# Differential heads: one VectorE instruction for the first softmax's scaling and the sum of both

## The chip, the cores and the metric

The kernel runs on one core of one Trainium2 chip. A core has five engines with a queue each: TensorE (PE in the profile; its weight loads are shown apart as PEld), VectorE (DVE), ScalarE (ACT), GpSimd (POOL) and SyncE (SP), which here issues most of the DMAs. Each engine works through its own instructions in a fixed order and waits on semaphores for the others.

The metric is the device time of one execution in microseconds (us); lower is better.

## The reference

The reference is one decoder block on a sequence of 1024 tokens with 1024 channels, float32. The input is normalised (RMS) and projected. Two attention branches follow: eight "forgetting" heads (FoX) of 64 channels, and four differential heads. Both are gated, merged by sigmoid gates, projected out, normalised and added to the input.

A differential head has two pairs of queries and keys, with rotary embedding, and one value of 128 channels. Its output is the difference of two causal softmaxes, times the value:

```
logits = einsum('bhmqd,bhmkd->bhmqk', qi, k) * scale        # m = 0, 1
p  = softmax(where(kpos <= qpos, logits, -inf))
pd = p[:, :, 0] - lam * p[:, :, 1]                          # lam: one number per layer
out = einsum('bhqk,bhkd->bhqd', pd, v)
```

## The kernel before, in words

Matrix products are made in a high and a low part: each float32 operand is split into a rounded part and the remainder, and three products (high x high, high x low, low x high) are summed.

The kernel goes through five stages: it loads and transposes x and makes the values (to about 100 us of the span); it works through eight attention units, units 0 to 3 being the differential heads and 4 to 7 pairs of FoX heads; then gates, branch products and the output projection.

In an attention unit the 1024 queries are taken in eight blocks of 128, called rows here (i = 0 to 7), in groups of two (g). The groups of one unit go up or down in order (GORD). Row i of a differential head has n = (i + 1) x 128 columns, and goes through these steps:

- s_row (line 449), once for each of the two softmaxes: two matmuls per piece of up to 512 columns write the scores to a PSUM tile Sd (lines 460, 461; three such tiles take turns); a VectorE instruction (line 463) scales them, adds the mask, writes them to a row buffer Pd in SBUF and finds the maximum (mxd); ACT takes the exponential in place and sums it (line 469) into one column of a small tile l. The row buffers come from a pool of six.
- row (line 550): VectorE takes the reciprocals of both sums (line 559, tile l). POOL multiplies the second row p2 with its reciprocal and with nlam, which is -lam (line 560). ACT multiplies the first row p1 with its reciprocal (line 562). POOL adds p2 to p1 (line 563).
- av (line 473): TensorE transposes blocks of p1 (line 490, tile ptd), ACT copies the high part (line 493, phd), VectorE makes the low part (line 494, pld), and TensorE multiplies with the value (line 514, ypd).

FoX rows have one softmax each: reciprocal on VectorE (line 590), scaling on POOL (line 591), no sum.

Beside the rows, TensorE has filler work in the same stretch: the projections of the next unit's queries and keys (line 301, tiles pq and pk) and of gate paths (pz). These bring work for the other engines: splitting the weights (hi on POOL, line 289; lo on VectorE, line 291), and for differential heads the rotary embedding: a copy on ACT (line 339), four DMAs that swap halves (line 343), a product on VectorE (line 345), a product on POOL (line 346, swq and swk), their sum on VectorE (line 347, rotq and rotk), and the split into the tiles TA, TB, KA, KB on ACT and VectorE (lines 352 to 355).

The order of instructions on each engine isn't the order in which the code is written. A planner works it out when the program is built, by simulating it with its own costs: what was written first has priority, and an engine takes the first instruction that is ready. A few orders are pinned by hand (issue_after). On the chip the order of each engine is then fixed.

Of the kernel before, what the change touches and what calls it, by code (L numbers as in the profile page):

```python
# [11 lines left out]
AF = mybir.ActivationFunctionType  # L12
ALU = mybir.AluOpType
# [31 lines left out]
def f32(ap):  # L45
    return ap.bitcast(F32)
# [3 lines left out]
def tile_hybrid_block(  # L50
# [18 lines left out]
    nc = tc.nc  # L69
# [237 lines left out]
    with ExitStack() as st:  # L307
# [127 lines left out]
        def swapped(T, m, g, nm):  # L435

            src = T["TB" if m else "TA"]
            qs = slice(2 * g * P, (2 * g + 2) * P)
            t = qk.tile([P, 2 * P], F32R, tag=f"X{m}", name=f"X{m}{nm}_{g}", bufs=3)
            for a, b in ((UPR, DNR), (DNR, UPR)):  # L440
                lastx[0] = nc.sync.dma_start(f32(t[a]), f32(src[b, qs])).ins
            if vload:
                with tc.issue_after(lastx[0]):
                    vload.pop(0)()
            return t
# [3 lines left out]
        def s_row(T, m, i, X, bias, boff, nm, le=None):  # L449

            A, B = (T["TA"], T["KA"]) if m == 0 else (T["TB"], T["KB"])
            n = (i + 1) * P
            qs = slice(i * P, (i + 1) * P)
            xs = slice(i % 2 * P, (i % 2 + 1) * P)
            pr = pp.tile([P, S], F32, tag="P", name=f"P{nm}_{m}_{i}")
            mx = small.tile([P, 2], F32, tag="mx", name=f"mx{nm}_{m}_{i}", bufs=8)
            pcs = pieces(i)
            for j, (a, b) in enumerate(pcs):
                ps = sps.tile([P, CH], F32, tag="S", name=f"S{nm}_{m}_{i}_{j}")[:, 0:b - a]
                nc.tensor.matmul(ps, lhsT=A[:, qs], rhs=B[:, a:b], start=True, stop=False)  # L460
                lasts[0] = nc.tensor.matmul(  # L461
                    ps, lhsT=X[:, xs], rhs=B[:, a:b], start=False, stop=True).ins
                nc.vector.tensor_tensor_reduce(  # L463
                    out=pr[:, a:b], in0=ps, in1=bias[:, boff + a:boff + b], scale=-0.125,
                    scalar=BIG if j == 0 else mx[:, j - 1:j], op0=ALU.add, op1=ALU.min,
                    accum_out=mx[:, j:j + 1])
            if le is None:
                le = small.tile([P, 1], F32, tag="l", name=f"l{nm}_{m}_{i}", bufs=8)
            nc.scalar.activation(pr[:, 0:n], pr[:, 0:n], AF.Exp,  # L469
                                 bias=mx[:, len(pcs) - 1:len(pcs)], scale=-1.0, accum_out=le)  # L470
            return pr, le
# [57 lines left out]
        def unit_attn(u, T):  # L529

            diff = u < 4
            t = u if diff else u - 4
            vt = qk.tile([P, NB, 256], F32R, tag="V", name=f"V{u}")
            src = (vb_d if diff else va_d)[:, t, :].rearrange("(b p) c -> p b c", p=P)
            cb = []
            groups = []

            def load_v():
                nc.sync.dma_start(f32(vt), src)

            def load():
                if not diff:
                    for m in range(2):
                        b = big.tile([P, S], F32, tag="big", name=f"cb{u}_{m}")
                        h = 2 * t + m
                        nc.sync.dma_start(b, cum_d[h:h + 1, :].to_broadcast([P, S]))
                        cb.append(b)

            if diff:
                def row(i, rows):  # L550
                    boff = S - (i + 1) * P
                    if "X" not in rows:
                        rows["X"] = [swapped(T, m, i // 2, f"d{u}") for m in range(2)]
                    le = small.tile([P, 2], F32, tag="l2", name=f"l{u}_{i}", bufs=4)
                    l1, l2 = le[:, 0:1], le[:, 1:2]
                    p1, _ = s_row(T, 0, i, rows["X"][0], dmask, boff, f"d{u}", l1)
                    p2, _ = s_row(T, 1, i, rows["X"][1], dmask, boff, f"d{u}", l2)
                    n = (i + 1) * P
                    nc.vector.reciprocal(le, le)  # L559
                    nc.gpsimd.tensor_scalar(  # L560
                        p2[:, 0:n], p2[:, 0:n], l2, nlam, op0=ALU.mult, op1=ALU.mult)
                    nc.scalar.activation(p1[:, 0:n], p1[:, 0:n], AF.Copy, scale=l1)
                    nc.gpsimd.tensor_tensor(
                        p1[:, 0:n], p1[:, 0:n], p2[:, 0:n], op=ALU.add)
                    rows[i] = p1

                def evac(g):
                    def run(yp):
                        ys = stg.tile([P, 2 * P], F32, tag="ys", name=f"ys{u}_{g}")
                        nc.scalar.copy(ys, yp)  # L570
                        nc.sync.dma_start(y_d[u][:, g * 2 * P:(g + 1) * 2 * P], ys)
                    return run

                for g in GORD[u]:
                    rows = {}
                    groups.append((
                        4 * g + 3,
                        [lambda i=i, rows=rows: row(i, rows) for i in (2 * g, 2 * g + 1)],
                        lambda g=g, rows=rows: av(rows, g, vt, 0, False, evac(g), f"d{u}_{g}", False)))
            else:  # L580
                ysb = {}

                def row(m, i, rows):
                    n = (i + 1) * P
                    diag = cb[m][:, n - P:n]
                    nc.gpsimd.tensor_tensor(diag, diag, trim, op=ALU.add)  # L586
                    if "X" not in rows:
                        rows["X"] = swapped(T, m, i // 2, f"f{u}")
                    p1, l1 = s_row(T, m, i, rows["X"], cb[m], 0, f"f{u}")
                    nc.vector.reciprocal(l1, l1)  # L590
                    nc.gpsimd.tensor_scalar(  # L591
                        p1[:, 0:n], p1[:, 0:n], l1, 1.0, op0=ALU.mult, op1=ALU.mult)
                    rows[i] = p1

                def evac(m, g):
                    def run(yp):
                        if m == 0:
                            ysb[g] = stg.tile([P, 2 * P], F32, tag="ys", name=f"ys{u}_{g}")
                        tmp = stg.tile([P, 2 * P], F32, tag="yt", name=f"yt{u}_{m}_{g}", bufs=1)
                        nc.scalar.copy(tmp[64:128], yp[64:128])  # L600
                        nc.vector.tensor_tensor(
                            ysb[g][64 * m:64 * m + 64], yp[0:64], tmp[64:128], op=ALU.add)
                        if m == 1:
                            nc.sync.dma_start(y_d[u][:, g * 2 * P:(g + 1) * 2 * P], ysb[g])
                    return run

                for g in GORD[u]:
                    for m in range(2):
                        rows = {}
                        groups.append((  # L610
                            4 * g + 3,
                            [lambda m=m, i=i, rows=rows: row(m, i, rows) for i in (2 * g + 1, 2 * g)],
                            lambda m=m, g=g, rows=rows: av(
                                rows, g, vt, m * P, True, evac(m, g), f"f{u}_{m}_{g}",
                                u == 7 and g in FING)))
            return load, load_v, groups
# [528 lines left out]
```

## Time and profile before

| | |
|---|---|
| time of three runs, median (lowest to highest) | 905.3 us (904.18 to 906.15) |
| the profiled execution's own time | 906.41 us |
| its span, first to last instruction | 904.6 us |
| granted TensorE clock | 0.998 |
| busy: PE, DVE, ACT, POOL | 883.2, 606.5, 439.5, 421.6 us |
| differential rows (tile Pd), first and last start | 138.5 to 358.8 us |

The span is what the profile covers; 1.8 us of the execution lie outside it. Busy time is the time in which an engine works on instructions; ends of matmuls are modelled, so that a busy PE can still lose time between matmuls. In a row of a group, "x32 | 24.7, 774 | 10.3" means 32 instructions, 24.7 us in all, 774 ns on average, and 10.3 us in which the engine stood idle just before them, with what ended that idle time. "A <- B: 3.5, 4, 1.5" means that A waited for B 3.5 us in total, 4 times, at most 1.5 us. "128x512" is partitions by elements.

### The profile page before, as it was taken

The numbers are of one execution on the slowest core, as the hardware profiler recorded it, in microseconds if no ns is written. First come the engines' busy times: TensorE is split into PE (matmuls) and PEld (weight loads), VectorE is DVE, ScalarE is ACT, GpSimd is POOL, SyncE is SP. The second block draws the span as 40 slices with busy tenths as digits, with TensorE's granted clock in tenths as the row PEclk, the third lists the DMA queues.
The fourth block names the chain that finished last, engine by engine and source line by source line (L and its number), as shares of the span: only waits on it lengthen the run. The fifth ranks groups of instructions, "written<-read, shape, count | busy, mean of one in ns | idle before, by whom it ended". The sixth has DMA issues, their size and how long they took to land.

```text
span 904.6 us, 13660 instructions
## 1 busy us (share of the span) xinstructions
PE 883.2 (98%) x4600; PEld 746.0 (82%) x4600; DVE 606.5 (67%) x1150; ACT 439.5 (49%) x878; POOL 421.6 (47%) x413
## 2 busy tenths in 40 slices
PE   7999999899999999999999999999999999999996
PEld 5899988688888888888888888888888888888885
DVE  6767556878668664557657557526586896648797
ACT  3433225576757675365555547534444362314342
POOL 7325324545546456154344446425634323483861
PEclk9999999999999999999999999999999999999999
DMA  9556747424336350432523532198766599210395
GB/s 321 191 169 257 277 114 196 112 76 124 108 70 185 76 181 19 140 85 76 163 59 88 152 89 71 40 405 264 229 201 203 199 306 339 73 45 0 118 194 177
DMA packets 129224, 140.09 MB, mean 155 GB/s; under 512 B 10353, under 2 KB 96369, under 8 KB 128130
## 3 DMA queue, kind: packets, MB, share of 16 engines
q1 hardware_dynamic: 124786, 136.87, 48.2%
q0 software_dynamic: 4224, 2.10, 2.0%
q8 instruction: 36, 0.59, 0.3%
q14 instruction: 34, 0.28, 0.1%
q10 hardware_dynamic: 144, 0.26, 0.1%
HBM read 86.17 MB, written 38.34 MB: 138 GB/s over the span
## 4 chain that ended last, share of the span: by engine, by line
PE 84%; DVE 5%; issue 3%; POOL 3%; DMA 2%; ACT 2%; SPq 1%; POOLq 0%; DVEq 0%; ACTq 0%
PE x_g L785 15%; PE pb L945 10%; PE pv L200 9%; PE x_o L785 9%; PE pz L301 8%; PE pk L301 7%; PE pq L301 7%; PE ypf L514 4%; PE ptf L490 3%; PE ypd L514 2%; PE Sd L460 2%; PE Sf L460 2%; PE Sf L461 1%; PE ptd L490 1%; PE Sd L461 1%
## 5 line engine op out<-in xcount | busy, mean ns | idle before, releaser
L200 PE MATMUL pv<-wvhi,hT 128*128 128x264 f32 (+2 forms) x384 | 88.8, 323 | 0.4 <-DVE hT L186 0.4
L301 PE MATMUL pz<-hT,hi_z 128*128 128x512 f32 x256 | 83.5, 397 | 0.2 <-ACT sq L418 0.2
L301 PE MATMUL pk<-hT,hi_k 128*128 128x512 f32 x256 | 82.3, 395 | 0.9 <-DVE KB L355 0.9
L301 PE MATMUL pq<-hT,hi_q 128*128 128x512 f32 x256 | 81.8, 394 | 0.0
L945 PE MATMUL pb<-yT,hi_br 128*128 128x512 f32 x256 | 78.8, 389 | 0.0
L785 PE MATMUL x_g<-T,a_g 128*128 128x512 f32 x336 | 78.0, 391 | 0.0
L785 PE MATMUL x_o<-wo_op,a_o 128*128 128x512 f32 x336 | 77.6, 392 | 0.0
L785 PEld LDWEIGHTS x_o<-wo_op,a_o 128*128 128x128 f32 x336 | 63.0, 188 | 14.5 <-DVE a_o L735 0.5
L785 PEld LDWEIGHTS x_g<-T,a_g 128*128 128x128 f32 x336 | 63.1, 188 | 13.8
L200 PEld LDWEIGHTS pv<-wvhi,hT 128*128 128x128 f32 x384 | 64.2, 189 | 6.1 <-DVE hT L186 0.7
L469 ACT ACTIVATE Pd<-Pd,mxd 128x128 f32<-128x128 f32 (+7 forms) x64 | 49.6, 775 | 35.6 <-DVE mxd L463 35.3
L586 POOL TENSOR_TENSOR cb<-cb,trim 128x128 f32<-128x128 f32 x64 | 31.3, 492 | 70.2 <-DVE mxf L463 51.8
L200 PE MATMUL pv<-wvlo,hT 128*128 128x512 f32 (+2 forms) x192 | 62.0, 325 | 0.7 <-DVE wvlo L156 0.7
L494 DVE TENSOR_TENSOR plf<-ptf,phf 128x512 fp32r<-128x512 f32 (+1 forms) x80 | 50.0, 635 | 17.7 <-ACT phf L493 16.7
L469 ACT ACTIVATE Pf<-Pf,mxf 128x1024 f32<-128x1024 f32 (+3 forms) x64 | 49.8, 778 | 24.4 <-DVE mxf L463 23.5
L591 POOL TENSOR_SCALAR Pf<-Pf,lf 128x1024 f32<-128x1024 f32 (+3 forms) x64 | 47.9, 753 | 27.9 <-DVE lf L590 25.6
L560 POOL TENSOR_SCALAR Pd<-Pd,l,nlam 128x128 f32<-128x128 f32 (+7 forms) x32 | 29.3, 916 | 66.1 <-DVE l L559 59.9
L785 PE MATMUL x_g<-hT,a_g 128*128 128x512 f32 x252 | 59.1, 392 | 0.0
L945 PEld LDWEIGHTS pb<-yT,hi_br 128*128 128x128 f32 x256 | 48.1, 188 | 9.9
L785 PEld LDWEIGHTS x_g<-hT,a_g 128*128 128x128 f32 x252 | 47.3, 188 | 10.5
L301 PEld LDWEIGHTS pk<-hT,hi_k 128*128 128x128 f32 x256 | 47.2, 188 | 10.3 <-DVE KB L355 1.5
L301 PEld LDWEIGHTS pq<-hT,hi_q 128*128 128x128 f32 x256 | 47.6, 188 | 9.2
(261 smaller groups left out, 2339.3 us busy)
## 6 DMA issues: line engine op xcount, KB each, us to landing
t_d<-t SPq DMA_DIRECT2D x16, 512.0 KB, 4.2
T<-t_d SPq DMA_DIRECT2D x8, 1024.0 KB, 10.5
raw<-in_w_in_dram SPq DMA_DIRECT2D x14, 512.0 KB, 4.9
vb_d<-vbs SPq DMA_DIRECT2D x8, 512.0 KB, 3.8
va_d<-vas SPq DMA_DIRECT2D x8, 512.0 KB, 5.2
raw_k<-in_w_in_dram SPq DMA_DIRECT2D x8, 512.0 KB, 5.3
raw_q<-in_w_in_dram SPq DMA_DIRECT2D x8, 512.0 KB, 4.2
V<-vb_d SPq DMA_DIRECT2D x4, 1024.0 KB
```

The lines of the kernel that those rows point to most:

```text
L200: nc.tensor.matmul(ps[n], lhsT=hT[hp][k // 4][i // 4][:, k % 4, hs], rhs=wt[k][:, a:b], start=first, stop=(k == KT - 1 and hp == 1))
L301: mm = nc.tensor.matmul(ps, lhsT=a[:, k, :], rhs=hT[h][k // 4][c][:, k % 4, :], start=(k == 0 and a is hi and h == 0), stop=(k == KT - 1 a ...
L460: nc.tensor.matmul(ps, lhsT=A[:, qs], rhs=B[:, a:b], start=True, stop=False)
L469: nc.scalar.activation(pr[:, 0:n], pr[:, 0:n], AF.Exp, bias=mx[:, len(pcs) - 1:len(pcs)], scale=-1.0, accum_out=le)
L490: lasts[0] = nc.tensor.transpose(pt[:, o * P:(o + 1) * P], rows[2 * g + r][:, j * P:(j + 1) * P], ident).ins
L494: nc.vector.tensor_tensor(pl[:, 0:n], pt[:, 0:n], ph[:, 0:n], op=ALU.subtract)
L514: lasts[0] = nc.tensor.matmul(o, lhsT=a, rhs=b[:, src], start=(j == 0 and n == 0), stop=(odd == 1 and jj == g and n == len(prods) - 1)).ins
L560: nc.gpsimd.tensor_scalar(p2[:, 0:n], p2[:, 0:n], l2, nlam, op0=ALU.mult, op1=ALU.mult)
L586: nc.gpsimd.tensor_tensor(diag, diag, trim, op=ALU.add)
L591: nc.gpsimd.tensor_scalar(p1[:, 0:n], p1[:, 0:n], l1, 1.0, op0=ALU.mult, op1=ALU.mult)
L785: nc.tensor.matmul(x[m], lhsT=a[:, ai, k, :], rhs=right[m][bi][k], start=(k == 0 and n == 0), stop=(k == 3 and n == 2))
L945: nc.tensor.matmul(ps, lhsT=a[:, kk, :], rhs=yT[g][h][:, k % 2, sl], start=(k == 0 and a is hi and h == 0), stop=(k == 3 and a is lo))
```

## The change

The scaling of the first row on ACT and the sum on POOL are replaced by one scalar_tensor_tensor on VectorE, which multiplies p1 with its reciprocal and adds p2, in place in p1. The scaling of p2 on POOL stays, and so do the reciprocals. All four differential heads are affected, 32 rows in all.

```
                     nc.vector.reciprocal(le, le)
                     nc.gpsimd.tensor_scalar(
                         p2[:, 0:n], p2[:, 0:n], l2, nlam, op0=ALU.mult, op1=ALU.mult)
-                    nc.scalar.activation(p1[:, 0:n], p1[:, 0:n], AF.Copy, scale=l1)
-                    nc.gpsimd.tensor_tensor(
-                        p1[:, 0:n], p1[:, 0:n], p2[:, 0:n], op=ALU.add)
+                    nc.vector.scalar_tensor_tensor(
+                        p1[:, 0:n], p1[:, 0:n], l1, p2[:, 0:n], op0=ALU.mult, op1=ALU.add)
                     rows[i] = p1
```

## The prediction

> **What bounds the kernel now.** I read the page's busy times first, then busy times by stretch, then the waits of the matmul engine and of VectorE inside the stretch that the change touches.
>
> ```profile
> PE 883.2 (98%) x4600; PEld 746.0 (82%) x4600; DVE 606.5 (67%) x1150; ACT 439.5 (49%) x878; POOL 421.6 (47%) x413
> ```
>
> TensorE is busy for 98% of the span, the others for 47 to 67%. That is an average, so the next view is by stretch. The differential rows (tile Pd) run between 138 and 345 us. The columns are busy us and count for PE, PEld, DVE, ACT, POOL, then the granted clock.
>
> ```profile
> 140.00:360.00 220.00, 215.12 (x1154) 181.14 (x1154) 156.12 (x368) 141.97 (x288) 119.85 (x104) 1.00 0.43 114
> 160.00:180.00 20.00, 17.27 (x86) 13.39 (x85) 17.68 (x32) 10.34 (x19) 10.80 (x8) 1.00 0.46 116
> 260.00:280.00 20.00, 19.99 (x114) 16.96 (x113) 16.97 (x36) 11.73 (x24) 11.20 (x9) 1.00 0.47 126
> 360.00:580.00 220.00, 217.70 (x1272) 188.65 (x1271) 136.61 (x365) 123.39 (x270) 94.24 (x135) 1.00 0.34 97
> ```
>
> In the differential stretch PE is idle for 220 - 215.12 = 4.9 us, and 20 - 17.27 = 2.7 us of that lies in the one slice 160 to 180, the slice where VectorE is at 17.68 / 20 = 88%. Over the whole stretch VectorE is at 156.1 / 220 = 71%. So TensorE sets the end and VectorE is next. What PE waits for there (columns: us in total, times, longest):
>
> ```profile
> PE Sd L460 <- DVE mxd L463: 3.5, 4, 1.5
> PE pk L301 <- DVE KB L355: 0.9, 1, 0.9
> PE ptd L490 <- POOL Pd L563: 0.4, 1, 0.4
> ```
>
> 4.4 of its 4.8 us are waits for VectorE, 0.4 us for the POOL sum that the change removes. PE does not wait for the ACT scaling at all. Whatever the change frees on POOL and ACT can therefore give back at most 4.8 us here, and only by way of VectorE.
>
> **What is removed.** 32 scalings on ACT and 32 sums on POOL, one of each for every differential row.
>
> ```profile
> L562 ACT ACTIVATE Pd<-Pd,l 128x128 f32<-128x128 f32 (+7 forms) x32 | 24.7, 774 | 10.3 <-DVE l L559 10.2
> L563 POOL TENSOR_TENSOR Pd<-Pd,Pd 128x128 f32<-128x128 f32 (+7 forms) x32 | 48.1, 1508 | 8.7 <-ACT Pd L562 5.9 <-issue 1.6
> L560 POOL TENSOR_SCALAR Pd<-Pd,l,nlam 128x128 f32<-128x128 f32 (+7 forms) x32 | 29.3, 916 | 66.1 <-DVE l L559 59.9 <-PE pz L301 4.3 <-ACT Pd L469 1.9
> ```
>
> ACT loses 24.7 us of 142.0, POOL 48.1 us of 119.9. Neither is close to full in this stretch and PE waits for neither, apart from the 0.4 us, so by themselves these 72.8 us are worth 0.4 us. What covers them is the matmul stream (215 of 220 us); without that cover a row's own path would count: after the reciprocal it is now max(916, 774) + 1508 = 2.42 us on average until the transposes may read the row.
>
> **What is added.** 32 scalar_tensor_tensor instructions on VectorE, widths 128 to 1024, both tensor inputs in SBUF. The stretch has none, but other stages have them at 128x512:
>
> ```profile
> L1071 DVE SCALAR_TENSOR_TENSOR go<-go,ors,mg 128x512 f32<-128x512 f32 x4 | 2.8, 747 | 1.1 <-POOL ors L1055 1.1
> L176 DVE SCALAR_TENSOR_TENSOR xg<-xs,rs,g_bc 128x512 f32<-128x512 f32 x16 | 13.2, 859 | 2.9 <-POOL rs L118 2.9
> L463 DVE CUSTOM_DVE_ANT_0 Pd<-Sd,dmask 128x512 f32<-128x512 f32 x32 | 21.8, 682 | 3.3 <-POOL Pd L563 1.9 <-PE Sd L461 1.3
> L463 DVE CUSTOM_DVE_ANT_0 Pd<-Sd,dmask 128x384 f32<-128x384 f32 x16 | 8.7, 551 | 4.9 <-PE Sd L461 3.6 <-POOL Pd L563 1.2
> ```
>
> The two widths of L463 differ by 682 - 551 = 131 ns for 128 columns. From 747 ns at 512 columns I get 354 ns at 128, 485 at 256, 616 at 384, 878 at 640 and 1271 at 1024: eight widths together 6.5 us, four heads 26.0 us, mean 812 ns. L176's mean instead of L1071's would add 32 x 0.11 = 3.6 us; I take L1071, the row nearest to L463's 682 ns for the same width, and price POOL's disturbance separately below. No DMA is issued, removed or moved by the change, so no queue of SP or POOL is passed. A row's path becomes 916 + 812 = 1.73 us, 0.7 us shorter, if VectorE is free when POOL is done.
>
> The Trainium skill (Vector Engine (DVE) Microarchitecture Reference, Points that are easy to get wrong) says that this instruction shape with two SBUF sources that are not bf16 runs at half throughput. L1071 has just such sources (go and mg are f32 in SBUF) and takes 747 ns against 682 ns for L463, which reads one input from PSUM: no halving here. By the rule the sum would be 52 us in place of 26.0 us.
>
> **VectorE against POOL.** Instructions of VectorE with two SBUF inputs get longer when POOL is already working. The rows, in order of time (start us, us):
>
> ```profile
> 151.66 0.69 DVE L355 TENSOR_TENSOR KB<-rotk,KB 64x512 fp32r<-64x512 f32 x1
> 155.23 1.49 DVE L347 TENSOR_TENSOR rotq<-rotq,swq 128x512 f32<-128x512 f32 x1 [1.48 <-POOL swq L346]
> 160.31 1.07 DVE L353 TENSOR_TENSOR TA<-rotq,TA 64x512 fp32r<-64x512 f32 x1
> 168.54 1.94 DVE L355 TENSOR_TENSOR KB<-rotk,KB 64x512 fp32r<-64x512 f32 x1
> ```
>
> ```profile
> 155.15 1.03 POOL L563 TENSOR_TENSOR Pd<-Pd,Pd 128x384 f32<-128x384 f32 x1
> 156.13 1.50 POOL L289 TENSOR_SCALAR hi_z<-raw_z 128x1024 fp32r<-128x1024 f32 x1
> 158.92 1.92 POOL L563 TENSOR_TENSOR Pd<-Pd,Pd 128x512 f32<-128x512 f32 x1 [0.31 <-ACT Pd L562]
> 167.96 1.97 POOL L563 TENSOR_TENSOR Pd<-Pd,Pd 128x640 f32<-128x640 f32 x1 [1.25 <-ACT Pd L562]
> ```
>
> Undisturbed it is 0.69 us (151.66). At 168.54 KB overlaps a POOL sum that ends at 169.93 and itself ends 0.55 us after that. So the second one stands until the first is done, and the POOL sums cost VectorE 0.80 + 0.38 + 1.25 = 2.43 us in this stretch alone. The new instruction comes under the same lock. It starts at the end of a POOL scaling, where POOL may have its next instruction ready and take the lock again. The nearest rows are the rope sums, also two-input instructions released by POOL:
>
> ```profile
> L347 DVE TENSOR_TENSOR rotk<-rotk,swk 128x512 f32<-128x512 f32 x8 | 7.9, 990 | 14.2 <-POOL swk L346 14.2
> L347 DVE TENSOR_TENSOR rotq<-rotq,swq 128x512 f32<-128x512 f32 x8 | 7.6, 946 | 9.0 <-POOL swq L346 9.0
> ```
>
> Their mean is 968 ns against 690, so 0.28 us each: 32 x 0.28 = 9.0 us for the new instructions at most by these rows, nothing at least. I take the upper end as nearest. The Trainium skill (SBUF — State Buffer, Who interferes with whom) calls it an exclusive lock between a VectorE instruction with two SBUF inputs and a GpSimd instruction that reads SBUF; by that rule, the trace agrees, it speaks against a change that puts 32 more such instructions on VectorE.
>
> **Waits that go and come.** VectorE itself waits in this stretch for the removed sum, because the sum holds the second softmax's buffer:
>
> ```profile
> DVE Pd L463 <- POOL Pd L563: 7.7, 4, 3.2
> DVE cum L646 <- POOL Pd L563: 1.4, 1, 1.4
> ```
>
> These 9.1 us end, for VectorE is then itself the last reader. In their place it waits for the POOL scaling L560, with the next rows' L463 reductions queued behind the waiting instruction, and PE's score matmuls behind those. The matching handoffs POOL to VectorE are the rope waits, 14.2 + 9.0 us over 16, mostly late DMA; the bound for 32 new waits is zero to 32 x 0.92 = 29 us (0.92 is L560's own time, as if VectorE always came at its start). I take near zero: the order of each engine is planned with the POOL scaling ahead.
>
> **The sum.** VectorE's work in the stretch goes from 156.1 to about 156.1 + 26.0 + 9.0, less the locks of the sums that go. That is near 186 to 191 us of 220, or 85 to 87%, like the slice 160 to 180 and the slice 260 to 280. Most of it falls where PE has matmuls to go on with. The place where VectorE leads PE is 155 to 171 us. There the rows of 384, 512 and 640 columns add 0.62 + 0.75 + 0.88 = 2.24 us and 3 x 0.28 = 0.84 us of lock; the locks of the sums give back 2.43 us (1.6 us if hi_z moves up and takes the first). With the 0.4 us that PE waited for the sum: 2.24 + 0.84 - 2.43 - 0.4 = +0.25 us, on the profiled execution's 906.4 us. That execution is 1.1 us above the median of 905.3 us, so the forecast is 905.6 us: no change that can be told (about 0.2%, or 1.8 us, is what a measurement of this kernel can tell).
>
> **Rivals.**
>
> *The freed POOL and buffer shorten the chain (faster).* The chain of waits around 193 to 219 us runs through the removed pair:
>
> ```profile
> 192.28 1.06 ACT Pd L562
> 193.48 2.39 POOL Pd L563
> ...
> 207.94 0.75 POOL Pd L563
> ...
> 217.39 1.27 POOL Pd L563
> ```
>
> Together 5.47 us; the new instructions for these widths (1024, 256, 512) take 1.27 + 0.49 + 0.75 = 2.5 us, 3.0 us less. For it: the 9.1 us of VectorE's buffer waits end as well. Against it: PE waited only 0.4 us for that chain. Time 905.3 - 3.0 = 902.3 us, at the very best 905.3 - 4.8 = 900.5 us.
>
> *VectorE becomes the bound (slower).* The place is 140 to 219 us, where that chain is mostly off PE. The price: twelve rows, one whole head and the first four of the next, put 6.5 + 2.2 = 8.7 us on VectorE, with 12 x 0.28 = 3.4 us of lock; the pieces above give back 5.47 us, so 8.7 + 3.4 - 5.47 = +6.6 us, or +4.2 us with the sums' locks (2.43 us) given back too. It decides once a scalar_tensor_tensor stands in VectorE's queue ahead of a reduction that PE's next score matmul waits for. For it: 3.5 of PE's 4.8 us are of this kind. Against it: in the slice 260 to 280 VectorE is at 16.97 / 20 = 85% and PE loses 0.01 us. Time 909.5 to 911.9 us.
>
> *The instruction runs at half rate (slower).* Each takes twice the time worked out from L1071, 8.7 us more in the same twelve rows: 905.3 + 4.2 + 8.7 = 918.2 us. L1071 itself speaks against it; 2%. It is what the Trainium skill's page on the VectorE microarchitecture, cited above, would make of the change.
>
> *The planner.* The order on each engine is worked out from the planner's own costs, so other lines move too, also behind the stretch, where 220 - 217.70 = 2.3 us of PE idle is all there is to win. This can blur each case by about 2 us either way.
>
> **How the numbers follow.** No change 36%, the chain shortened 30%, VectorE as the bound 32%, half rate 2%. That gives faster 0.30, same 0.36, slower 0.34. The likeliest's own range is 903.5 to 907.1 us; signs being nearly even, the range reaches to the best case, 900.5 us, and to the second's upper price, 911.9 us.
>
> **What would show it.** A group of 32 scalar_tensor_tensor on Pd at 0.81 us undisturbed, up to 1.09 us with locks; POOL busy in the stretch down by 48 us, ACT by 25 us, VectorE up by 26 to 35 us less 2 to 8 us; no wait of L463 for a POOL sum; PE's idle time in 140 to 360 still near 5 us. I am wrong if that idle time goes under 3 us or over 8 us, if VectorE's waits for L560 exceed 10 us, or if the stretches behind 360 us change by more than 2 us.

## The result, and the profile after

The changed kernel takes 914.48 us in the median of six runs (910.29 to 916.85), beside 905.67 us of six runs of the kernel before (904.18 to 908.15). The ratio is 1.0081, with a 95% interval from 1.0062 to 1.0100: slower. The ratio comes from the comparison of the runs and isn't quite the quotient of the two medians. Where I turn a ratio into us below, I multiply what it has over 1 by 905.8 us, a median of the kernel before: here +7.3 us (5.6 to 9.1). The profiled execution took 912.89 us, of which the span is 911.1 us, 6.5 us more than before. One of the ten runs of e4, an experiment below, took 2043.86 us, more than twice any other, and is left out of its median and ratio.

The page's busy times after, then busy times by stretch (columns as before: PE, PEld, DVE, ACT, POOL, granted clock):

```profile
PE 887.9 (97%) x4600; PEld 747.7 (82%) x4600; DVE 627.3 (69%) x1182; ACT 417.1 (46%) x846; POOL 373.9 (41%) x381
```

```profile
140.00:360.00 220.00, 212.58 (x1127) 176.75 (x1126) 173.52 (x392) 116.06 (x253) 70.52 (x68) 1.00 0.42 113
360.00:580.00 220.00, 217.98 (x1264) 188.40 (x1262) 136.64 (x363) 124.02 (x269) 95.74 (x138) 1.00 0.34 97
```

In the differential stretch POOL lost 119.85 - 70.52 = 49.3 us, ACT 25.9 us, and VectorE gained 17.4 us. Behind 360 us nothing moved. So the loss lies inside the stretch, and little of it shows as idle time of TensorE: its idle time over the whole span grew from 904.6 - 883.2 = 21.4 to 23.2 us, only 1.8 us. Its busy time grew by 4.7 us, with the same 4600 matmuls. Ends of matmuls are modelled, so a matmul that starts late can have a longer record, and small gaps vanish in it. To find the place I therefore compared starts. In each trace the matmuls were added up in order, each by its undisturbed spacing (0.227 us at 512 columns, 0.117 at 256, 0.060 at 128), and I looked at when each kernel had started the same amount of work:

```
work done before at (us)   34   137   158   183   205   249   270   292   315   337   537   end
after behind by (us)     +1.4  +1.4  +1.8  -0.5  -0.9  +0.6  +0.4  +4.9  +6.0  +6.4  +6.2  +6.5
```

The 1.4 us at 34 us are not the change: up to about 130 us the two have the same order of instructions, and other runs differ by as much there. In the first differential head the changed kernel even gains 2.3 us. By 270 us it is level. It then loses 5.6 us within 45 us, and hardly anything more. At 297 us, where the kernel before begins its fourth differential head, it is already 6.1 us behind, so the loss lies in the third. Busy times of the four heads, each from its first reciprocals (line 559) to the next head's, first before, then after:

```profile
146.00:201.00 55.00, 51.75 (x265) 41.76 (x264) 42.58 (x92) 34.26 (x69) 30.93 (x25) 1.00 0.46 119
201.00:246.00 45.00, 44.62 (x245) 38.20 (x244) 33.54 (x81) 30.42 (x64) 23.54 (x21) 1.00 0.44 117
246.00:297.00 51.00, 50.08 (x276) 42.60 (x275) 39.40 (x92) 34.48 (x73) 28.95 (x25) 1.00 0.45 118
297.00:344.00 47.00, 46.67 (x258) 39.73 (x257) 28.69 (x75) 32.16 (x65) 25.08 (x23) 1.00 0.42 120
```

```profile
147.00:204.00 57.00, 55.06 (x284) 45.50 (x283) 48.68 (x101) 29.41 (x61) 19.54 (x18) 1.00 0.46 119
204.00:256.00 52.00, 51.13 (x275) 42.92 (x274) 41.48 (x94) 27.79 (x64) 16.30 (x15) 1.00 0.39 105
256.00:303.00 47.00, 42.81 (x235) 34.76 (x233) 39.14 (x93) 26.04 (x58) 13.84 (x15) 1.00 0.45 120
303.00:350.00 47.00, 46.58 (x255) 39.37 (x254) 34.83 (x81) 24.37 (x53) 14.94 (x16) 1.00 0.42 120
```

TensorE's idle time in the third head goes from 0.92 to 4.19 us, while the first head's falls from 3.25 to 1.94 us. VectorE does not explain it by its share alone: in the third head it is at 39.14 / 47 = 83%, in the first at 48.68 / 57 = 85%. What differs is what TensorE has beside the rows. The projections alone (line 301; columns PE, PEld, clock), in the same heads, before and then after:

```profile
146.00:201.00 55.00, 37.73 (x145) 26.45 (x146) 1.00 0.46 119
201.00:246.00 45.00, 30.01 (x118) 21.32 (x117) 1.00 0.44 117
246.00:297.00 51.00, 32.82 (x128) 23.05 (x127) 1.00 0.45 118
297.00:344.00 47.00, 27.07 (x111) 20.14 (x110) 1.00 0.42 120
```

```profile
147.00:204.00 57.00, 42.40 (x163) 29.70 (x163) 1.00 0.46 119
204.00:256.00 52.00, 33.79 (x132) 23.68 (x130) 1.00 0.39 105
256.00:303.00 47.00, 23.36 (x89) 16.14 (x90) 1.00 0.45 120
303.00:350.00 47.00, 27.38 (x113) 20.37 (x111) 1.00 0.42 120
```

The number of projection matmuls goes 145, 118, 128, 111 before and 163, 132, 89, 113 after. With longer rows the planner fits more of them between the rows of the first two heads, and the third head is left with 39 fewer, 9.5 us of TensorE's work (its window is 4 us shorter, too). The third unit is the one that has none of the gate projection as filler of its own. A list in the kernel says which of its eight parts go to which unit:

```
ZFILL = ((0,), (1,), (), (2,), (3,), (4,), (5,), (6, 7))
```

There the chain of each row shows. The three longest waits of TensorE's matmuls in 280 to 303 us, in order of time (start us, us), and instructions of VectorE ahead of the first:

```profile
285.70 0.50 PE L460 MATMUL Sd<-KA,TA 128*128 128x512 f32 x1 [1.16 <-DVE mxd L463]
299.64 0.30 PE L490 MATMUL ptd<-ident,Pd 128*128 128x128 f32 x1 [0.95 <-DVE Pd L562]
300.60 0.39 PE L460 MATMUL Sd<-KB,TB 128*128 128x256 f32 x1 [0.66 <-DVE mxd L463]
```

```profile
280.83 0.89 DVE L562 SCALAR_TENSOR_TENSOR Pd<-Pd,l,Pd 128x640 f32<-128x640 f32 x1 [1.08 <-POOL Pd L560]
284.31 0.93 DVE L347 TENSOR_TENSOR rotq<-rotq,swq 128x512 f32<-128x512 f32 x1 [1.98 <-POOL swq L346]
285.16 0.47 DVE L463 CUSTOM_DVE_ANT_0 Pd<-Sd,dmask,mxd 128x256 f32<-128x256 f32 x1
```

The score matmuls (L460) wait for VectorE's reduction (L463) to release the PSUM tile, and the transposes (L490) for the new instruction. VectorE in turn has stood idle for POOL. Not all of that is the new instruction's doing. The reduction that the matmul of 285.70 us waits for stands behind a sum of the rotary embedding (L347, a rope sum), which waited 1.98 us for POOL's rope product, and that one 2.19 us for its DMA:

```profile
282.99 1.29 POOL L346 TENSOR_TENSOR swq<-swq,sinT 128x512 f32<-128x512 f32 x1 [2.19 <-DMA swq<-rawq]
```

By starts, 2.1 of the 5.6 us are lost just here (+1.3 us at 282 us, +3.4 us at 286). The kernel before (its rope sum at 281.74 us) and e1 and e3 below don't wait at this place; e5 waits 1.95 us. Whether the order or the DMA brings this wait was not tested.

The group of the new instruction in 138 to 365 us after:

```profile
L562 DVE SCALAR_TENSOR_TENSOR Pd<-Pd,l,Pd 128x128 f32<-128x128 f32 (+7 forms) x32 | 34.2, 1069 | 10.6 <-POOL Pd L560 10.4
```

The 32 new instructions take 34.2 us, 1069 ns each, and VectorE stands 10.4 us before them waiting for the POOL scaling, 13 times and at most 1.5 us. Some are long for the lock with POOL, as foreseen. This one, 128x1024 (1.27 us by the forecast's row), starts just behind a product of POOL:

```profile
194.26 2.32 DVE L562 SCALAR_TENSOR_TENSOR Pd<-Pd,l,Pd 128x1024 f32<-128x1024 f32 x1
```

```profile
194.20 1.30 POOL L346 TENSOR_TENSOR swk<-swk,sinT 128x512 f32<-128x512 f32 x1 [0.92 <-DMA swk<-rawk]
```

### The profile page after: what moved, and what is told of

Same layout as the page of the kernel before. It is cut to its first block, busy times and chain, and to the rows that moved or that the text cites. A ratio compares the mean times of both kernels' runs of the same rounds, so it can differ in the third digit from the quotient of the medians.

```text
span 911.1 us, 13604 instructions
## 1 busy us (share of the span) xinstructions
PE 887.9 (97%) x4600; PEld 747.7 (82%) x4600; DVE 627.3 (69%) x1182; ACT 417.1 (46%) x846; POOL 373.9 (41%) x381
## 4 chain that ended last, share of the span: by engine, by line
PE 82%; DVE 5%; DMA 3%; issue 3%; ACT 2%; SPq 2%; POOL 1%; DVEq 0%; POOLq 0%; ACTq 0%
PE x_g L784 15%; PE pv L200 10%; PE pb L944 10%; PE x_o L784 8%; PE pz L301 8%; PE pk L301 7%; PE pq L301 7%; PE ypf L514 3%; PE ptf L490 3%; PE ypd L514 2%; DMA swq<-rawq 2%; PE Sf L460 1%; PE Sf L461 1%; PE pg L301 1%; PE ptd L490 1%
## 5 line engine op out<-in xcount | busy, mean ns | idle before, releaser
L200 PE MATMUL pv<-wvhi,hT 128*128 128x264 f32 (+2 forms) x384 | 90.7, 328 | 0.8 <-DVE hT L186 0.8
L493 ACT CAST phf<-ptf 128x512 fp32r<-128x512 f32 (+1 forms) x80 | 42.6, 542 | 38.0 <-PE ptf L490 31.7
```

The costliest lines, as they stand in the source:

```text
L200: nc.tensor.matmul(ps[n], lhsT=hT[hp][k // 4][i // 4][:, k % 4, hs], rhs=wt[k][:, a:b], start=first, stop=(k == KT - 1 and hp == 1))
L493: nc.scalar.copy(ph[:, 0:n], pt[:, 0:n])
```

## The experiments

The theories were these. LOAD: VectorE's extra work costs time where TensorE has too little filler, whatever the work is. HANDOFF: VectorE stands behind POOL, first for the scaled p2 and then for the lock. HOLE: the place is the third head, because its unit has no gate filler; in the texts written before the runs this goes by the name of COVER, against LOAD EVERYWHERE, by which the loss follows VectorE's work wherever the filler stands. ORDER: adding instructions upsets the planner's order, and their work doesn't matter. All kernels were timed beside the kernel before:

| run | edit | median, us | before, us | ratio (95%) |
|---|---|---|---|---|
| changed kernel | | 914.48 | 905.67 | 1.0081 (1.0062 to 1.0100) |
| e1 | before + load on VectorE | 911.76 | 905.77 | 1.0070 (1.0052 to 1.0088) |
| e2 | before + load behind POOL | 918.26 | 905.77 | 1.0135 (1.0119 to 1.0152) |
| e3 | after, POOL's scaling last | 913.37 | 905.77 | 1.0080 (1.0055 to 1.0106) |
| e4 | after, p2 scaled on ACT | 908.69 | 905.77 | 1.0022 (1.0007 to 1.0038) |
| e5 | after, filler in third unit | 909.45 | 905.97 | 1.0044 (1.0029 to 1.0058) |
| e6 | before, filler in third unit | 905.97 | 905.97 | 1.0002 (0.9986 to 1.0017) |
| e7 | after, hole in second unit | 911.98 | 905.97 | 1.0069 (1.0046 to 1.0092) |
| e8 | e4, filler in third unit | 905.27 | 905.97 | 0.9999 (0.9980 to 1.0017) |
| e9 | e3, filler in third unit | 905.89 | 905.72 | 0.9995 (0.9983 to 1.0007) |
| e10 | e4, hole in seventh unit | 911.29 | 905.72 | 1.0059 (1.0044 to 1.0073) |
| e11 | before, hole in seventh unit | 914.44 | 905.72 | 1.0092 (1.0073 to 1.0110) |
| e12 | after, hole in seventh unit | 916.04 | 905.72 | 1.0115 (1.0092 to 1.0137) |
| e13 | e1, filler in third unit | 906.34 | 906.38 | 1.0002 (0.9989 to 1.0016) |
| e14 | e2, filler in third unit | 909.21 | 906.38 | 1.0030 (1.0016 to 1.0043) |
| e15 | before + one-column products | 908.29 | 906.38 | 1.0020 (1.0005 to 1.0035) |

In e1, e2 and e13 to e15 the added instructions write a column that nobody reads. Nothing of the computation is left out in any of them; e3, e4 and those built on them compute the same sum with its factors in other places.

**Load alone, and load behind POOL (e1, e2).** Both leave ACT's scaling and POOL's sum as they were and add 32 sums over n columns on VectorE, in e1 right behind the reciprocals with an input that is there from the start, in e2 behind POOL's scaling of p2. The small tile le is widened for their results.

```
 e1:
-                    nc.vector.reciprocal(le, le)
+                    rec = nc.vector.reciprocal(le[:, 0:2], le[:, 0:2]).ins
+                    with tc.issue_after(rec):
+                        nc.vector.tensor_reduce(
+                            out=le[:, 4:5], in_=dmask[:, 0:n], axis=mybir.AxisListType.X, op=ALU.add)
 e2, behind the POOL scaling:
+                    nc.vector.tensor_reduce(
+                        out=le[:, 4:5], in_=p2[:, 0:n], axis=mybir.AxisListType.X, op=ALU.add)
```

> The kernel before with 32 extra sums over the mask tile on VectorE, one behind each pair of reciprocals, 128 to 1024 columns wide, that nothing waits for (about 24 us of VectorE work, no POOL wait, no second SBUF input). Theory LOAD (VectorE's added busy time is what PE loses): 911 to 915 us. Theory HANDOFF (VectorE standing still behind POOL's scaling, with the next reductions queued behind it): 905 to 908 us. Theory ORDER (the planner's new order happens to be a worse one): anything from 903 to 915 us, with no relation to the load.

> As e1_load_only, but each of the 32 sums reads the second row after POOL has scaled it, so VectorE has to wait for POOL; the row itself still goes by ACT and the POOL sum. LOAD: the same as e1_load_only within 1.5 us. HANDOFF: 4 to 7 us slower than e1_load_only, with about 10 us of VectorE waits for the POOL scaling. ORDER: no relation to e1_load_only.

e1 costs 6.3 us (4.7 to 8.0), nearly all that the change costs, with no wait of VectorE for POOL's scaling and nothing taken from ACT or POOL. It is level with before at 270 us (+0.0), 0.6 us behind at 292 and 4.0 at 297: the same head, though later in it. There a score matmul of TensorE (296.62 us, shown in the last section) waits 2.49 us for a reduction that stands behind the added sum and two more instructions in VectorE's queue:

```profile
293.39 1.07 DVE L561 TENSOR_REDUCE l<-dmask 128x1 f32<-128x896 f32 x1
294.49 0.69 DVE L353 TENSOR_TENSOR TA<-pq,TA 64x512 fp32r<-64x512 f32 x1
295.10 0.67 DVE L353 TENSOR_TENSOR KA<-pk,KA 64x512 fp32r<-64x512 f32 x1
295.80 0.75 DVE L463 CUSTOM_DVE_ANT_0 Pd<-Sd,dmask,mxd 128x512 f32<-128x512 f32 x1
```

About 2.5 of the 6.3 us are TensorE's clock, which falls after such waits (last section). e2 costs 12.2 us. Its group rows of 1024 columns, with e1's behind them, show that the added instruction itself is the same, 1215 against 1198 ns:

```profile
L562 DVE TENSOR_REDUCE l<-Pd 128x1 f32<-128x1024 f32 x4 | 4.9, 1215 | 0.1
```

```profile
L561 DVE TENSOR_REDUCE l<-dmask 128x1 f32<-128x1024 f32 x4 | 4.8, 1198 | 0.0
```

What e2 has more is this row of its waits, 12.3 us in 16 waits, at most 1.3 us:

```profile
DVE l L562 <- POOL Pd L560: 12.3, 16, 1.3
```

So standing behind POOL costs 5.9 us more (1.0135 - 1.0070), and there without any lock: the sums read one input, and they do not get longer. Part of it may go by way of the filler again: e2's third head has 83 projection matmuls, e1's 91. The Trainium skill (SBUF — State Buffer, Who interferes with whom) says that this instruction never contends with GpSimd on trn2; the 1215 ns agree.

**POOL's part put elsewhere (e3, e4).** e3 forms p1 + p2 x (l1 x nlam / l2) on VectorE first and lets POOL multiply by 1 / l1 afterwards, so that VectorE waits for no POOL work. Its reciprocals go to columns 2 and 3 of le. e4 keeps the changed kernel's instruction and lets ACT scale p2, with nlam folded in by a one-column product.

```
 e3:
-                    nc.gpsimd.tensor_scalar(p2, p2, l2, nlam, ...)
-                    nc.vector.scalar_tensor_tensor(p1, p1, l1, p2, mult, add)
+                    nc.vector.scalar_tensor_tensor(ra, le[:, 3:4], nlam, l1, mult, mult)
+                    nc.vector.scalar_tensor_tensor(p1, p2, ra, p1, mult, add)
+                    nc.gpsimd.tensor_scalar(p1, p1, le[:, 2:3], 1.0, ...)
 e4:
-                    nc.gpsimd.tensor_scalar(p2, p2, l2, nlam, ...)
+                    nc.vector.tensor_tensor(l2, l2, nlam, mult)
+                    nc.scalar.activation(p2, p2, AF.Copy, scale=l2)
```

> The changed kernel with the two steps in the other order: VectorE first combines the rows with one small ratio per query (second reciprocal times -lam times first sum), then POOL scales the result. The same 32 wide instructions on VectorE and 32 scalings on POOL, plus 32 tiny ones on VectorE, the same result; but VectorE no longer waits for POOL. LOAD: 912 to 916 us, like the changed kernel. HANDOFF: 904 to 908 us. ORDER: anything from 903 to 915 us.

> The changed kernel with the second row scaled on ACT in place of POOL (ACT is freed of the first row's scaling, so its work is that of the kernel before), plus 32 tiny products on VectorE. VectorE waits for ACT, and POOL has no row work left, so nothing of the rows holds the lock between POOL and VectorE. LOAD: 911 to 915 us. HANDOFF in the wide sense (any engine in front): 910 to 914 us with 8 us or more of VectorE waits for ACT. If it is POOL alone, by lock and lateness: 904 to 908 us, and the wide instruction at 0.85 us on average in place of 1.07. ORDER: anything from 903 to 915 us.

The group of the new instruction in e3 and then in e4, in 138 to 365 us:

```profile
L563 DVE SCALAR_TENSOR_TENSOR Pd<-Pd,l,Pd 128x128 f32<-128x128 f32 (+7 forms) x32 | 27.6, 865 | 0.7
```

```profile
L562 DVE SCALAR_TENSOR_TENSOR Pd<-Pd,l,Pd 128x128 f32<-128x128 f32 (+7 forms) x32 | 27.7, 875 | 7.2 <-ACT Pd L561 7.2
```

The lock is nearly gone in both (27.6 and 27.7 us, against 34.2), and in e3 the wait is gone too. Yet e3 costs 7.2 us, as much as the changed kernel: HANDOFF as the sole cause falls. Both also have 32 one-column instructions on VectorE, 9.0 us in e3 and 6.6 us in e4, so that e3 loads VectorE no less than the changed kernel does. e4 costs 2.0 us (0.6 to 3.4), less than LOAD expected, and at 908.69 us just above what was expected if POOL alone counted. Its load on VectorE is within 2.4 us of e3's, and its third head has about as many projection matmuls (95 in 254 to 300 us, e3 92 in 254 to 299), so neither tells them apart. I have not settled where this difference comes from.

**The hole (e5, e6, e7).** e5 and e6 move one part of the gate projection from the fourth unit to the third, with the changed row and with the row before. e7 moves another from the second to the third, so that the second has none.

```
 before:      ZFILL = ((0,), (1,), (), (2,), (3,), (4,), (5,), (6, 7))
 e5, e6:      ZFILL = ((0,), (1,), (2,), (), (3,), (4,), (5,), (6, 7))
 e7:          ZFILL = ((0,), (), (1,), (2,), (3,), (4,), (5,), (6, 7))
```

> The changed kernel with one gate projection (48 matmuls of 0.227 us, 10.9 us of TensorE work) moved from the fourth differential head to the third, which has none of its own. Theory COVER (VectorE's load costs only where TensorE has too little filler, in the third head: 93 projection matmuls against 128 to 135 in the first two): 904 to 908 us, PE idle in the third head under 2 us in place of 4.2. Theory LOAD EVERYWHERE (the loss follows VectorE's work, wherever the filler stands): 911 to 916 us, the loss showing in the fourth head instead. ORDER: anything from 903 to 916 us.

> The same move in the kernel before, as a control. COVER: 903.5 to 906 us, since the third head lost only about 1 us there. LOAD EVERYWHERE: 905 to 907 us. ORDER: anything from 902 to 910 us.

> The changed kernel with the second head's gate projection moved to the third head, so that the second head is the one without. COVER: the loss moves with the hole: PE idle of 3 us or more between about 205 and 255 us, under 2 us in the third head; 909 to 916 us in all. LOAD EVERYWHERE: the loss stays in the third head or spreads, 911 to 916 us. ORDER: no relation to the hole.

The 93 and 128 to 135 projection matmuls of the first text were counted in somewhat other windows than the 89, 163 and 132 above. For the kernel before the place of that part makes no difference (1.0002). For the changed one it is worth 3.4 us of its 7.3 (5.0 by the medians); at 909.45 us e5 lies between the two ranges, and TensorE's idle time in its third head is 2.1 us, where HOLE had less than 2.

e7 failed both of HOLE's signs: TensorE is idle for 1.8 us in 205 to 255 us, not for 3 or more, and for 2.9 us in the third head (261 to 301 us), not for less than 2. The hole didn't move as I meant. The planner drew 31 of the moved part's 48 matmuls forward, so that the second head has 152 projection matmuls and the third 70, fewer than the 89 of the changed kernel. The loss goes with these counts: e7 stands at -1.7 us at 228 us, near the end of the second head at -0.2 (257 us), and at +4.3 us at 297 us, where the kernel before ends the third. That fits HOLE, but only once the counts were known.

**Filler under each kind of load (e8, e9, e13, e14).** The list of e5 with e4, e3, e1 and e2.

> e4_act_p2 (second row scaled on ACT, nothing of the rows on POOL) with the gate projection moved to the third head. COVER: 903 to 906 us. LOAD EVERYWHERE: 907 to 911 us as without the move. ORDER: anything from 902 to 912 us.

> e3_scale_after (VectorE combines first, POOL scales behind it, so no VectorE wait for POOL) with the gate projection moved to the third head. What is left of the loss in e5_after_z2 (+3.5 us) is in question. If it is VectorE's wait for POOL's scaling and the lock on the wide instruction: 904.5 to 907 us. If COVER leaves a part of the load unpaid: 908 to 911 us, as in e5_after_z2. ORDER: no relation to either.

> e1_load_only (32 extra sums over the mask on VectorE, that nothing waits for) with the gate projection moved to the third head. If filler covers pure load: 904.5 to 907.5 us in place of 911.8. If load costs by itself: 910 to 912 us. ORDER: 903 to 912 us.

> e2_load_handoff (the extra sums wait for POOL's scaling) with the gate projection moved to the third head. If the wait for POOL has its own price behind cover: 3 to 6 us above e13_load_only_z2. If cover pays for the wait too: within 1.5 us of e13_load_only_z2. ORDER: no relation to e13_load_only_z2.

This is the clearest result. Load without a wait for POOL costs nothing that can be told once there is filler: e13 is at 1.0002, e9 at 0.9995 and e8 at 0.9999, where the same rows without it cost 6.3, 7.2 and 2.0 us. The third head of e1 and then of e13 (each from the first reciprocals to the next head's), for each all instructions and then the projections alone:

```profile
254.00:300.00 46.00, 42.97 (x244) 37.44 (x243) 39.72 (x88) 31.13 (x66) 24.46 (x23) 0.97 0.44 121
```

```profile
254.00:300.00 46.00, 23.69 (x91) 16.39 (x90) 0.97 0.44 121
```

```profile
253.00:301.00 48.00, 48.00 (x268) 41.67 (x267) 39.50 (x89) 33.03 (x69) 27.73 (x25) 1.00 0.53 146
```

```profile
253.00:301.00 48.00, 33.11 (x127) 22.88 (x125) 1.00 0.53 146
```

VectorE has the same work in both, 39.72 and 39.50 us. With 91 projection matmuls TensorE is idle for 3.0 us, with 127 for none. The fourth head of e13, now the one without a part, still has 109, and VectorE is busy there for only 32.76 of 47 us (301 to 348 us). Load with a wait for POOL keeps a cost under filler: e14 is 2.5 us above e13 (1.0030 - 1.0002; the two intervals just touch, and 3 to 6 us were expected), and the changed row is 4.4 us above e3's (e5 - e9: 1.0044 - 0.9995). In e5 VectorE waits as the following rows say, and the lock is there as in the changed kernel:

```profile
DVE Pd L562 <- POOL Pd L560: 7.4, 11, 1.1
```

```profile
L562 DVE SCALAR_TENSOR_TENSOR Pd<-Pd,l,Pd 128x128 f32<-128x128 f32 (+7 forms) x32 | 34.2, 1069 | 7.6 <-POOL Pd L560 7.4
```

It isn't the waiting as such. In e8 the same instruction waits longer, for ACT, and the kernel is level with the one before:

```profile
DVE Pd L562 <- ACT Pd L561: 10.4, 13, 1.5
```

In e5 the lock comes on top, but e14's sums have no lock. What makes the wait for POOL dear is not shown.

**The hole among the FoX heads (e10, e11, e12).** Every part from the third on moves one unit forward, so that the seventh unit, a pair of FoX heads, has none. There the rows are as before.

```
 ZFILL = ((0,), (1,), (2,), (3,), (4,), (5,), (), (6, 7))
```

> e8_act_p2_z2 with a gate projection in the fourth head as well (each later one moved one head forward, the seventh unit is left with none). In e8_act_p2_z2 the fourth head was left without and lost about 2.5 us, the clock record showing a stretch at half clock there. COVER: 902 to 905 us. If the move only carries the hole to a FoX unit that needs it as much: 905 to 908 us. ORDER: 902 to 910 us.

> The kernel before with the same filler as e10_act_p2_z3, as its control. COVER: 904 to 906.5 us, no difference that can be told, since VectorE isn't the bound there. ORDER: 902 to 910 us.

> The changed kernel with the same filler. COVER: 906 to 909.5 us, no slower than e5_after_z2 (909.5). If the cover is only shifted: 910 to 914 us. ORDER: 903 to 914 us.

All three came out slower than I expected: 5.3, 8.3 and 10.4 us over the kernel before. Up to 537 us e11 is level with it (-0.1 us); at 561 us it is 6.7 us behind, and e10 and e12 lose about 6 and 5 us at the same place. The stretch 550 to 570 us, before and in e11, for each all instructions and then the projections alone:

```profile
550.00:570.00 20.00, 19.54 (x128) 16.81 (x126) 14.12 (x45) 14.41 (x32) 12.27 (x16) 1.00 0.20 54
550.00:570.00 20.00, 4.59 (x21) 3.66 (x20) 1.00 0.20 54
```

```profile
550.00:570.00 20.00, 17.94 (x109) 13.37 (x108) 17.98 (x56) 15.12 (x31) 12.47 (x19) 1.00 0.11 28
550.00:570.00 20.00, 0.00 (x0) 0.00 (x0) 1.00 0.11 28
```

I had taken it that the FoX rows, without the added work, carry the hole. They don't: with 21 projection matmuls in this stretch the unit loses nothing, with none it loses TensorE time by its own row work. The third differential head before had no such loss; 128 projection matmuls were still there.

**The order alone (e15).** One-column products behind the reciprocals, 32 in all:

```
+                    nc.vector.tensor_tensor(le[:, 4:5], l1, l2, op=ALU.mult)
```

> The kernel before with 32 products of one column on VectorE behind the reciprocals (about 0.15 us each, 5 us in all), which move the planner's order but hardly load any engine. ORDER: more than 2 us away from the kernel before, in either direction. Otherwise: 905 to 907.5 us.

1.8 us (0.5 to 3.2) lies between what the theories expected. It isn't nothing, but it isn't the order alone either, for the products load VectorE with 12.9 us in place of 5. Half of them take 160 ns or less, about as expected. The twelve that take more than 260 ns all start while POOL is at work and end within 0.04 us of its instruction's end, so they stand under the lock, like this one:

```profile
176.37 1.80 DVE L560 TENSOR_TENSOR l<-l 128x1 f32<-128x1 f32 x1
```

```profile
176.08 2.08 POOL L564 TENSOR_TENSOR Pd<-Pd,Pd 128x768 f32<-128x768 f32 x1 [0.17 <-ACT Pd L563]
```

The loss of the third head is not in it: at 270 us this kernel is 1.0 us behind, at 337 us 1.1 us. This reordering doesn't make the 7.3 us; that no other order could is not shown.

## Why the prediction was wrong, point by point

The forecast was 905.6 us, no change; 914.48 us was measured, 2.6 us above the top of the range.

- *What bounds the kernel, and what the removed work is worth.* Right. POOL lost 49.3 us and ACT 25.9 us in the stretch (48 and 25 predicted), and the time did not fall by it.
- *The size of the new instruction.* Right. 26.0 us without locks and at most 9.0 us of them were predicted. Undisturbed ones took 0.74 us at 512 columns and 1.27 us at 1024, as worked out. With nearly no lock all 32 take 27.6 us (e3), with it 34.2 us, of 35.0. The half-rate rival is out: it would have been 52 us.
- *VectorE's load.* It gained 17.4 us in 140 to 360 us, against 26 to 35 less 2 to 8, that is 18 to 33: a little below. But that window holds less of the work after than before; over the whole span VectorE gained 627.3 - 606.5 = 20.8 us, which is inside. Since the new instructions take 34.2 us, VectorE's other work got 13.4 us shorter, more than the 2 to 8 us forecast; 8.5 us of that are the sums and splits of the rotary embedding (rotk, TA, TB, KA, KB), the kind that the removed POOL sums held up.
- *The step that failed: "Most of it falls where PE has matmuls to go on with. The place where VectorE leads PE is 155 to 171 us."* It took the cover from a whole stretch, and from the order before. By the counts the filler is one supply for all four heads: with longer rows more of it goes into the first two (163 and 132 instead of 145 and 118), and the third runs short (89 instead of 128). At 155 to 171 us nothing was lost to speak of; by its end the first head had gained. Nearly all of the loss came in 270 to 297 us, in a head where TensorE was idle for 0.92 of 51 us before. A similar load costs 6.3 us without that cover and nothing that can be told with it (e1, e13). For the changed row itself the cover is worth 3.4 of 7.3 us (e5).
- *The second step that failed: VectorE's wait for POOL's scaling, "I take near zero".* It was 10.4 us in 13 waits. The bounds, 0 to 29 us, held it, the choice didn't, and the 10 us that I had named as the mark of being wrong was passed. By e14 over e13 such waits cost 2.5 us under filler, and by e2 over e1 5.9 us without. With filler, and with VectorE's wait for POOL gone, the change costs nothing that can be told (e9).
- *The rival that VectorE becomes the bound.* Its mechanism was the right one in the main: score matmuls wait for reductions that come late in VectorE's queue. In e1 the added sum stands ahead of the reduction (293.39 us above); in the changed kernel a rope sum does at 285.70 us, and at 299.64 us a transpose waits for the new instruction itself. Its price, 4.2 to 6.6 us, holds e1's 6.3 and is below the 7.3 of the changed kernel. That it comes so near is in part luck, for the price was added up for other rows, and a part of e1's cost is the clock, which the price leaves out. Its place was wrong, 140 to 219 us, and my evidence against it was a slice of exactly the head that later failed: in 260 to 280 VectorE was at 85% and TensorE lost 0.01 us, but with its filler still there.
- *The freed POOL and buffer shorten the chain.* The waits of L463 for the POOL sum are gone. The 2.3 us gained in the first head (158 to 183 us) are not theirs for certain: e1, which keeps the pair, gains 1.4 us between the same points.
- *What would show it.* TensorE's idle time in 140 to 360 us is 220 - 212.58 = 7.4 us, under the 8 us that I had set. That mark was badly chosen: over the whole span TensorE's busy time grew by 4.7 us and its idle time by 1.8.

No version that was tried beats the kernel before: e8 and e9, which keep VectorE's instruction, cover the third head and take POOL out of VectorE's way, are level with it. What remains open is why e4 costs 5 us less than e3 without filler, what makes VectorE's wait for POOL dearer than its wait for ACT, and what brings the rope wait ahead of 285.70 us.

## What to carry to other kernels

Before work is added to an engine that is not the bound, follow the bound engine's filler through the stages: count it by stage, and ask which stage runs out first once each stage takes longer. A slice that shows 85% busy without loss is evidence for that amount of filler and no other. An instruction that waits for another engine and holds up the queue behind it can cost more than its length, as it did behind POOL here and didn't behind ACT. Neither remedy was enough alone: POOL's scaling moved last cost 7.2 us (e3), filler for the third head 4.0 (e5); with both (e9) the cost was gone.

## What the runs showed of the hardware

TensorE's granted clock fell to half after stalls that are much shorter than I expected to matter. In e1 TensorE waited 2.49 us for VectorE:

```profile
296.62 0.38 PE L460 MATMUL Sd<-KA,TA 128*128 128x256 f32 x1 [2.49 <-DVE mxd L463]
...
300.27 0.61 PE L301 MATMUL pk<-hT,lo_k 128*128 128x512 f32 x1
300.70 0.65 PE L301 MATMUL pk<-hT,hi_k 128*128 128x512 f32 x2
```

```profile
295.00:305.00 10.00, 8.38 (x34) 7.07 (x35) 7.08 (x23) 7.26 (x18) 7.04 (x6) 0.83 0.18 44
```

At 300.27 us the next matmul of 512 columns comes after 0.43 us instead of 0.23, and the granted clock of the slice is 0.83: (1 - 0.83) x 10 = 1.7 us lost, or 3.4 us at half speed. e3 and e4 show the same once (0.83 and 0.85 in 295 to 305 us), amid waits of 1.55 and 0.90 us and of 0.78 and 1.08 us, e8 in its fourth head (0.83 in 325 to 335 us) behind waits of 0.86 and 0.45 us, and e2 twice as long (0.87 in 295 to 305 us and 0.79 in the next 10). The changed kernel's profiled execution shows none of it (1.00 in the third head), and neither does the kernel before at 160 to 180 us, where TensorE is idle for 2.7 us. So waits of about 0.5 to 2.5 us sometimes cost 1.7 us more.

For executions that were not profiled the mean granted clock of each run gives an estimate. e1's four runs have 0.9955 on average and the kernel before beside them 0.9982, so 0.0027 x 910 = 2.5 us of e1's 6.3 are the clock, and its other stalls the rest. The changed kernel's six runs have 0.9973 on average, which by the same reckoning makes 0.8 us of its 7.3. With filler e13 is at 0.9981.

The Trainium skill (TensorE: Matmul & The Clock Gate, Why this matters for your kernels) asks for no idle gaps over some 3 us; the 3.4 us at half speed agree with the window that its Part 1 gives, but here gaps under 3 us were enough: 2.49 us in e1, and no single one over 0.9 us shortly before it in e8.
